# Attention with scores laid out key by query, the maximum brought in as a row of the product, and two heads on halves of TensorE's array

## The chip, the cores and the metric

The kernel runs on one core of a Trainium2 chip. The time is device microseconds (us) of one launch, median of several executions. Five engines work side by side: TensorE (PE; its loads of the stationary operand are listed as PEld), VectorE (DVE), ScalarE (ACT), GpSimd (POOL) and SyncE (SP), which issues the DMAs. TensorE multiplies a stationary operand of up to 128 contraction rows by 128 columns with a moving operand of up to 512 columns; the result lands in PSUM, in banks of 512 f32 per partition.

## The reference

A backbone of two layers over 512 latent tokens and 256 context tokens, width 1024, all in float32. Layer 0 mixes tokens by attention, layer 1 by a two-directional state-space scan; a gated convolutional feed-forward follows each. The change lies in the attention of layer 0. There are 16 heads of 64 channels and 4 key and value heads, so four query heads share one key head:

```python
def gqa_attend(q, k, v):
    s = jnp.einsum('bqhgd,bkhd->bhgqk', q, k).astype(jnp.float32) * (HEAD_DIM ** -0.5)
    p = jax.nn.softmax(s, axis=-1).astype(v.dtype)
    return jnp.einsum('bhgqk,bkhd->bqhgd', p, v)
```

Queries and keys are normalised per head, and those of latent tokens are rotated by position. The 512 latent queries attend to all 768 keys, the 256 context queries to the 256 context keys. An output projection `w_o` and a gated residual follow.

## The kernel before, in words

Activations lie channel major (channels on partitions, tokens along the free dimension). Float32 products are made from a fast, rounded format (fp32r): an operand is split into a rounded high part and a low rest (`split`, L81), and a product takes three passes, high x high, high x low, low x high (`mm3`, L100). Plain f32 products, used where the operand is not split, appear in the trace as two instructions each.

`attention` (L379) first makes queries, keys and values of the first heads in an order written out by hand, up to some 90 us. From `man.__exit__` on, the order of instructions on each engine is made by a planner: it takes the program's order as priority and, where an instruction would have to wait in its own timing, puts a later one first that is ready.

The attention proper runs over eight pairs of heads, and for each pair over three units (`Unit`): queries 0 to 255, 256 to 511 of the latents, and the context queries. A unit goes through two sets of steps, and the second set of one unit is written beside the first set of the next:

- `a_steps`: for each head `e` and each tile of 128 queries, `score` (L594) makes scores with queries on partitions and 768 (or 256) keys along the free dimension. The query operand holds the high part of a head on 64 rows and its low part on the other 64 (L562 to L566). The keys are there with their high part on both halves, and with their low part on both halves, so two passes give all four products. `softmax` (L570) takes the maximum along the row (L572), the exponential with that bias and its sum (L574), the reciprocal (L575), and scales (L576).
- `b_steps`: for each tile of 128 keys, four transposes on TensorE (L626) turn the probabilities so that keys lie on partitions; a copy out of PSUM on ScalarE or VectorE (L630); and the product with the values (L638), plain f32, one head on array columns 0 to 63 and one on 64 to 127. At the end the output is copied (L640) into a tile `o` that stays in SBUF for every pair.

Score results use the two PSUM buffers `S` of two banks each; all else uses four buffers `B` of one bank.

Between the steps `fill.run(us)` (L185) issues filling: other work that attention does not need at once, as generators that yield their cost. These are the conditioning products of layer 0 (`ada`, L111, which load 512 KB pieces of `in_adaB`), the preparation of queries of later pairs (`queries`, `normed`: product, rotation through a DMA that swaps partitions, L519, on SP, and GpSimd or VectorE, then normalisation), the second half of the keys, and, towards the end, the output projection of the first five pairs (`project`). A generator that yields `BREAK` is left alone for five calls and booked with 1.0 us. `fill.require` makes a preparation complete at that place. `osplit` splits a pair's output into its parts for the projection.

All DMAs go through SP's queue in its order; the time from issue to landing is listed in the profile.

## Time and profile before

| what | value |
|---|---|
| median of 3 runs | 1963.2 us (1959.49 to 1968.46) |
| the profiled execution | 1956.99 us, its span 1955.2 us |
| mean granted TensorE clock | 0.994 |
| score products (L594), first and last start | 94.6 and 396.3 us |
| value products (L638), first and last start | 121.9 and 418.4 us |
| busy time of L594, L626, L638 on TensorE, 92 to 425 us | 74.55, 74.92, 75.46 us |

Spans of a matrix product in the trace contain its pipeline, so that consecutive ones overlap; the distance of starts says how long one holds the engine. An entry `128*64 128x256 f32` is a product with 128 contraction rows, 64 columns of the array and 256 moving columns. In lists of groups, the number behind the bar is busy time and the mean of one instruction in ns, and then the idle time ahead of it with what ended it. In lists of waits, the columns are total us, times, longest.

### The profile page before, as it was taken

The page shows a single profiled execution, that of the slowest core. Times are in us where ns is not written, and L with a number is a line of the kernel's source. Part 1 is how long each engine was busy: PE and PEld are TensorE (multiplying, and loading weights), DVE is VectorE, ACT ScalarE, POOL GpSimd, SP SyncE. Part 2 cuts the span into 40 slices and gives each one's busy share as a digit, 9 for nine tenths or more (in the row PEclk, how much of TensorE's full clock was granted, in tenths as well). Part 3 has the DMA queues.
Part 4 walks back from the last instruction along what each step waited for, and adds up shares of the span by engine and source line. Part 5 has one row for each costly group of instructions (what it writes and reads, how often), then busy time and mean ns, then how long its engine had stood idle before and what let it go on. Part 6 is the DMA issues. An engine that isn't in the chain of part 4 may idle for free.

```text
span 1955.2 us, 28359 instructions
## 1 busy us (share of the span) xinstructions
PE 1909.6 (98%) x11068; PEld 1595.4 (82%) x11068; DVE 1346.6 (69%) x2119; ACT 885.1 (45%) x1636; POOL 297.5 (15%) x272
## 2 busy tenths in 40 slices
PE   8999999998999999999999999999999999999999
PEld 6866776688888888888888888888888888888887
DVE  4557778667877777775568777778878566555555
ACT  3645676436222222222256767666667343333331
POOL 2212201003000000000031233422335210000000
PEclk8999999999999999999999999999999999999999
DMA  8254010012434333332222433433354323333332
GB/s 330 87 183 162 28 33 17 1 55 98 143 125 123 128 124 123 123 106 65 76 87 66 134 119 108 121 116 92 103 162 119 101 74 96 97 97 97 97 98 87
DMA packets 71702, 205.36 MB, mean 105 GB/s; under 512 B 8720, under 2 KB 14224, under 8 KB 71440
## 3 DMA queue, kind: packets, MB, share of 16 engines
q1 hardware_dynamic: 71568, 203.54, 32.5%
q8 instruction: 87, 1.43, 0.3%
q14 instruction: 47, 0.39, 0.1%
HBM read 196.43 MB, written 4.46 MB: 103 GB/s over the span
## 4 chain that ended last, share of the span: by engine, by line
PE 70%; DVE 12%; issue 8%; POOL 4%; ACT 1%; DMA 1%; SPq 0%; POOLq 0%; DVEq 0%; ACTq 0%
PE ps_up L106 10%; PE ps_up L108 10%; PE ps_up L105 10%; PE ps_d L105 6%; PE ps_d L108 6%; PE ps_d L106 6%; PE ps_o L638 3%; PE ps_pt L626 3%; PE ps_s L594 2%; DVE xf L900 2%; POOL E L999 1%; DVE ht L281 1%; PE ps_in L108 1%; DVE E L1009 1%; DVE Bf L900 1%
## 5 line engine op out<-in xcount | busy, mean ns | idle before, releaser
L87 DVE TENSOR_TENSOR wl<-wst,wh 128x1024 fp32r<-128x1024 f32 x205 | 253.1, 1234 | 276.1 <-PE ps_up L106 124.1
L85 ACT CAST wh<-wst 128x1024 fp32r<-128x1024 f32 x211 | 221.1, 1049 | 413.3 <-DMA wst<-in_wup 323.7
L106 PE MATMUL ps_up<-hlf,wh 128*128 128x512 f32 x1008 | 357.0, 354 | 0.0
L105 PE MATMUL ps_up<-hhf,wh 128*128 128x512 f32 x1008 | 356.9, 354 | 0.0
L108 PE MATMUL ps_up<-hhf,wl 128*128 128x512 f32 x1008 | 356.8, 354 | 0.0
L106 PEld LDWEIGHTS ps_up<-hlf,wh 128*128 128x128 f32 x1008 | 190.6, 189 | 26.1
L105 PEld LDWEIGHTS ps_up<-hhf,wh 128*128 128x128 f32 x1008 | 190.5, 189 | 26.2
L108 PEld LDWEIGHTS ps_up<-hhf,wl 128*128 128x128 f32 x1008 | 190.5, 189 | 26.0
L105 PE MATMUL ps_in<-hhs,wh 128*128 128x512 f32 (+1 forms) x560 | 205.0, 366 | 0.0
L108 PE MATMUL ps_in<-hhs,wl 128*128 128x512 f32 (+1 forms) x560 | 199.7, 357 | 0.0
L106 PE MATMUL ps_in<-hls,wh 128*128 128x512 f32 (+1 forms) x560 | 199.5, 356 | 0.0
L105 PE MATMUL ps_d<-hdh,wh 128*128 128x512 f32 (+1 forms) x568 | 193.8, 343 | 1.4 <-DVE X L726 1.2
L108 PE MATMUL ps_d<-hdh,wl 128*128 128x512 f32 (+1 forms) x568 | 193.5, 341 | 0.0
L106 PE MATMUL ps_d<-hdl,wh 128*128 128x512 f32 (+1 forms) x568 | 193.0, 340 | 0.3 <-DVE hdl L87 0.3
L726 DVE SCALAR_TENSOR_TENSOR X<-ps_d,mod,X 128x512 f32<-128x512 f32 (+1 forms) x240 | 133.0, 584 | 31.3 <-PE ps_d L108 30.6
L106 PEld LDWEIGHTS ps_d<-hdl,wh 128*128 128x128 f32 x568 | 106.7, 188 | 15.5 <-DVE hdl L87 0.7
L105 PEld LDWEIGHTS ps_d<-hdh,wh 128*128 128x128 f32 x568 | 106.3, 188 | 15.3 <-DVE X L726 1.6
L105 PEld LDWEIGHTS ps_in<-hhs,wh 128*128 128x128 f32 x560 | 106.3, 190 | 15.1 <-issue 0.9
L108 PEld LDWEIGHTS ps_in<-hhs,wl 128*128 128x128 f32 x560 | 106.2, 190 | 14.9
L108 PEld LDWEIGHTS ps_d<-hdh,wl 128*128 128x128 f32 x568 | 106.7, 188 | 13.3
L106 PEld LDWEIGHTS ps_in<-hls,wh 128*128 128x128 f32 x560 | 106.3, 190 | 13.6
L167 DVE SCALAR_TENSOR_TENSOR junk<-wada,cb 128x1024 f32<-128x1024 f32 x96 | 116.7, 1215 | 1.1 <-ACT cb L159 0.9
(325 smaller groups left out, 3699.7 us busy)
## 6 DMA issues: line engine op xcount, KB each, us to landing
wst<-in_wup SPq DMA_DIRECT2D x88, 512.0 KB, 3.5
wada<-in_adaT SPq DMA_DIRECT2D x48, 512.0 KB, 3.5
wst<-in_win SPq DMA_DIRECT2D x48, 512.0 KB, 3.5
wst<-in_wdown SPq DMA_DIRECT2D x44, 512.0 KB, 4.1
wada<-in_adaB SPq DMA_DIRECT2D x32, 512.0 KB, 7.4
E<-ad SPq DMA_DIRECT2D x64, 256.0 KB, 6.5
ec<-ead SPq DMA_DIRECT2D x64, 128.0 KB, 4.3
wst<-in_wout SPq DMA_DIRECT2D x16, 512.0 KB, 3.5
```

The source lines that it names most:

```text
L85: keep(nc.scalar.copy(hi, src))
L87: keep(eng.tensor_tensor(lo, src, _r(hi), ALU.subtract))
L105: mm(out, wh, ah, start=first, stop=False)
L106: mm(out, wh, al, start=False, stop=False)
L108: mm(out, wl, ah, start=False, stop=last)
L167: g.tc.keep_in_program_order(nc.vector.scalar_tensor_tensor(junk, w, 1.0, cb[:, v * D : (v + 1) * D], ALU.mult, ALU.mult, accum_out=md[:, ...
L281: nc.vector.scalar_tensor_tensor(t[:, c0:c1], ap, g.moda[layer][ca][:, m, v : v + 1], rs[:, c0:c1], ALU.mult, ALU.mult)
L594: nc.tensor.matmul(ps[:, c0 : c0 + n], qprep[self.p][e][:, q0 : q0 + P], kk[:, self.k0 + c0 : self.k0 + c0 + n], start=i == 0, stop=i == 1)
L626: nc.tensor.transpose(ps[:, e * 256 + t * P : e * 256 + (t + 1) * P], self.pr[e, t][:, kt * P : (kt + 1) * P], g.ident)
L638: nc.tensor.matmul(po[S64[e], :256], v, pts[kt - 1][:, e * 256 : (e + 1) * 256], start=kt == 1, stop=kt == nkt)
L726: nc.vector.scalar_tensor_tensor(ap, o[:, c0:c1], gate[:, m, v : v + 1], ap, ALU.mult, ALU.add)
L900: nc.vector.scalar_tensor_tensor(cv, raw[:, tap : tap + n], par(f"sw{tap}", j), cv, ALU.mult, ALU.add)
```

## The change

Pairs are no longer cut into units. Each pair takes seven steps (`Pair.steps`), and each step makes scores with keys on partitions and queries along the free dimension: six tiles of 128 keys by 512 latent queries, and in the seventh step two tiles of context keys by 256 context queries. The two heads of the pair lie on rows 0 to 63 and 64 to 127 of the array (contraction over 64 channels), each writing its own PSUM bank; three passes (high keys x high queries, low x high, high x low). A fourth product per head, of one contraction row, adds the negative maximum of each query, which lies as a row `mrow` on partition 0 or 64. The exponential then needs no bias, one instruction takes both heads (128x1024), and its result serves the value product as it is. The sum over keys is added up on VectorE over steps and finished by a product with ones (`final`); the output is divided by it through logarithm, exponential and one correction step.

The maxima come from a pass of their own (`Pair.maxima`), written among the steps of the pair before: scores with queries on partitions from the high parts alone, the two heads again on halves of the rows, a maximum over 1024 elements, and then DMAs on SP that write the column of maxima to DRAM and read it back as a row on one partition. For the first pair it is written among the products of the values.

Queries are split into two full tiles `qh`, `ql`. Outputs of the first six pairs are stored to DRAM and loaded again for `osplit`. The pool of general tiles has 18 instead of 27 buffers, with tags of their own for `pr`, `acc`, `mrow` and `o`, which at the start hold weight slabs. The order of the filling and its cost per call differ.

```diff
+    spare = [("pr", 3, 1024)] * 3 + [("acc", 1, 1024)] + [("mrow", 2, T)] * 2 + [("o", 2, T)] * 2
+    def slab_tile(name):
+        if not spare:
+            return t3(g, name, F32R)
+        tag, bufs, n = spare.pop(0)
+        return g.t3p.tile([P, n], F32R, tag=tag, bufs=bufs, name=name)[:, :W6]
...
-        slabs[k] = hi, lo = t3(g, "wsh", F32R), t3(g, "wsl", F32R)
+        slabs[k] = hi, lo = slab_tile("wsh"), slab_tile("wsl")
...
-        out = []
-        for e in range(2):
-            a = t3(g, f"q{p}{e}", F32R)
-            s, o = S64[e], S64[1 - e]
-            nc.scalar.copy(a[s], qs[s])
-            nc.vector.tensor_tensor(a[o], qs[s], _r(a)[s], ALU.subtract)
-            out.append(a)
-        qprep[p] = out
+        qprep[p] = t3(g, "qh", F32R), t3(g, "ql", F32R)
+        split(g, qs, *qprep[p])
...
-    def softmax(pr, ps):
-        mx = g.p.tile([P, 1], F32, tag="mx", bufs=4, name="mx")
-        nc.vector.reduce_max(mx, ps, axis=AX.X, negate=True)
-        sm = g.p.tile([P, 1], F32, tag="sm", bufs=4, name="sm")
-        nc.scalar.activation(pr, ps, AF.Exp, bias=mx, accum_out=sm)
-        nc.vector.reciprocal(sm, sm)
-        nc.vector.tensor_scalar(pr, pr, sm, None, ALU.mult)
...
+    onesr = g.const.tile([P, P], F32R, name="onesr")
+    nc.scalar.copy(onesr, g.ones)
+    small = lambda name, dt=F32: g.p.tile([P, 2, T // P], dt, tag="mx", bufs=6, name=name)
+    class Pair:
+        def __init__(self, p):
+            self.p, self.kv = p, p // 2
+            self.todo = []
+        def maxima(self):
+            qh, kh = qprep[self.p][0], k2[self.kv][0]
+            lat, ctx, mx = small("ma"), small("mb"), small("mx", F32R)
+            self.mrow = g.t3p.tile([P, T], F32R, tag="mrow", bufs=2, name=f"mrow{self.p}")
+            def scores(ts, k0, n, out):
+                ps = Sb("ps_m")
+                for i, t in enumerate(ts):
+                    for e in range(2):
+                        nc.tensor.matmul(ps[:, 512 * e + n * i : 512 * e + n * i + n], qh[S64[e], t * P : (t + 1) * P],
+                                         kh[S64[e], k0 : k0 + n], start=True, stop=True)
+                nc.vector.reduce_max(out[:, :, ts[0] : ts[-1] + 1], ps.rearrange("p (e t k) -> p e t k", e=2, k=n),
+                                     axis=AX.X, negate=True)
+            def row(t0, t1):
+                for e in range(2):
+                    dr = g.dp.tile([1, T], F32, tag="mrow", bufs=4, name="mrow_d")
+                    c = slice(t0 * P, t1 * P)
+                    nc.sync.dma_start(dr[0, c].rearrange("(t p) -> p t", p=P), _r(mx[:, e, t0:t1]))
+                    nc.sync.dma_start(_r(self.mrow[64 * e : 64 * e + 1, c]), dr[:, c])
+            for t in (0, 2):
+                scores((t,), 0, L, lat)
+                yield
+                scores((t + 1,), 0, L, lat)
+                yield
+                scores((t, t + 1), L, C, ctx)
+                yield
+            nc.vector.tensor_tensor(mx[:, :, :4], lat[:, :, :4], ctx[:, :, :4], ALU.min)
+            row(0, 4)
+            scores((4, 5), L, C, lat)
+            nc.vector.tensor_copy(mx[:, :, 4:], lat[:, :, 4:])
+            row(4, 6)
+            yield
+        def steps(self):
+            (qh, ql), (kh, kl) = qprep[self.p], k2[self.kv]
+            po = acc = None
+            o = g.t3p.tile([P, T], F32, tag="o", bufs=2, name=f"o{self.p}")
+            def values(po, pr, t, off, n, first, last):
+                v = vt[t][:, self.kv * HD : (self.kv + 1) * HD]
+                for e in range(2):
+                    nc.tensor.matmul(po[S64[e], :n], v, pr[:, 512 * e + off : 512 * e + off + n], start=first, stop=last)
+            def final(po, ps, acc, out):
+                n = out.shape[-1]
+                for e in range(2):
+                    nc.tensor.matmul(ps[S64[e], :n], g.ones[:, :HD], acc[:, n * e : n * e + n], start=True, stop=True)
+                y, u = t2("y")[:, :n], t2("u")[:, :n]
+                nc.scalar.activation(y, ps, AF.Ln)
+                nc.scalar.activation(y, y, AF.Exp, scale=-1.0)
+                nc.vector.tensor_tensor(out, po, y, ALU.mult)
+                nc.vector.scalar_tensor_tensor(u, ps, -1.0, y, ALU.mult, ALU.mult)
+                nc.vector.scalar_tensor_tensor(out, u, 2.0, out, ALU.add, ALU.mult)
+            def later_lat(po, pr, t, acc):
+                values(po, pr, t, 0, L, t == 0, t == 5)
+                if t == 5:
+                    final(po, Bk("ps_sum"), acc, o[:, :L])
+            def later_ctx(pr, acc):
+                pc = Bk("ps_oc")
+                for t in range(2):
+                    values(pc, pr, 4 + t, C * t, C, t == 0, t == 1)
+                final(pc[:, :C], pc[:, C:], acc, o[:, L:])
+                if self.p < 6:
+                    nc.sync.dma_start(odram[self.p], o)
+            prev = None
+            for t in range(7):
+                ps, pr = Sb("ps_s"), g.t3p.tile([P, 1024], F32, tag="pr", bufs=3, name="pr")
+                for q0, n, k0, off in (((0, L, t * P, 0),) if t < 6 else ((L, C, L, 0), (L, C, L + P, C))):
+                    q, k = slice(q0, q0 + n), slice(k0, k0 + P)
+                    outs = [ps[:, 512 * e + off : 512 * e + off + n] for e in range(2)]
+                    for i, (a, b) in enumerate(((kh, qh), (kl, qh), (kh, ql))):
+                        for e in range(2):
+                            nc.tensor.matmul(outs[e], a[S64[e], k], b[S64[e], q], start=i == 0, stop=False)
+                    for e in range(2):
+                        r = slice(64 * e, 64 * e + 1)
+                        nc.tensor.matmul(outs[e], onesr[r], self.mrow[r, q], start=False, stop=True)
+                nc.scalar.activation(pr, ps, AF.Exp)
+                if t == 0:
+                    po = Bk("ps_o")
+                elif t == 1:
+                    acc = g.t3p.tile([P, 1024], F32, tag="acc", bufs=1, name="acc")
+                    nc.vector.tensor_tensor(acc, prev, pr, ALU.add)
+                elif t < 6:
+                    nc.vector.tensor_tensor(acc, acc, pr, ALU.add)
                 else:
+                    acc = t2("accc")
+                    halves = pr.rearrange("p (e k q) -> p e k q", e=2, k=2)
+                    nc.vector.tensor_tensor(acc.rearrange("p (e q) -> p e q", e=2), halves[:, :, 0], halves[:, :, 1], ALU.add)
+                prev = pr
+                yield (lambda t=t, pr=pr, po=po, acc=acc: later_lat(po, pr, t, acc)) if t < 6 else (
+                    lambda pr=pr, acc=acc: later_ctx(pr, acc))
+            g.o.append(o)
...
+    odram = [g.dp.tile([P, T], F32, name=f"odram{p}") for p in range(6)]
...
     def osplit(p):
         hl_, hc_ = htiles(g, L, f"ol{p}"), htiles(g, C, f"oc{p}")
+        o = g.o[p]
+        if p < 6:
+            o = t3(g, f"od{p}")
+            nc.sync.dma_start(o, odram[p])
+        split(g, o[:, :L], *hl_)
+        split(g, o[:, L:T], *hc_)
+    adas = list(fill.q)
+    fill.q = [kgen if o == "k" else adas.pop(0) if o == "a" else qgen[int(o)] for o in "12a3a4ka5a6a7aaa"]
+    pairs = [Pair(p) for p in range(NH // 2)]
+    m = pairs[0].maxima()
+    for i, _ in enumerate(vals):
+        if i % 6 == 5:
+            next(m, None)
+            next(qgen[1], None)
+    for _ in m:
+        pass
+    late_step = None
+    for p in range(NH // 2):
+        m = iter(())
+        if p < 7:
+            fill.require(qgen[p + 1])
+            if p == 3:
                 fill.require(kgen)
+            m = pairs[p + 1].maxima()
+        us = .8 if p < 6 else 1.45
+        for t, todo in enumerate(pairs[p].steps()):
+            next(m, None)
+            fill.run(us)
+            if late_step:
+                late_step()
+            late_step = todo
+            if t == 0:
+                next(m, None)
+                if p == 6:
+                    for i in range(5):
+                        osplit(i)
+                    late()
+            if p == 7 and t == 3:
+                osplit(5)
+                osplit(6)
+            fill.run(us)
+    late_step()
...
-    g.t3p, g.n3 = pool("pa", pha), 27
+    g.t3p, g.n3 = pool("pa", pha), 18
+    g.dp = pool("adram", pha, space=bass.MemoryType.DRAM)
```

More of the change, by code (lines that the diff above doesn't have):

```diff
@@ L673, in attention @@
-    fill.q = [vals] + [kgen if o == "k" else adas.pop(0) if o == "a" else qgen[int(o)] for o in "a1aa2aa3aaa4k567"]
+    adas = list(fill.q)
+    fill.q = [kgen if o == "k" else adas.pop(0) if o == "a" else qgen[int(o)] for o in "12a3a4ka5a6a7aaa"]
     g.o = []
-    units = [Unit(p, hf) for p in range(NH // 2) for hf in range(3)]
-    for n in range(len(units) + 1):
-        A = units[n] if n < len(units) else None
-        B = units[n - 1] if n else None
-        if n == 1:
-            fill.q.remove(vals)
-            for i, _ in enumerate(vals):
-                if i % 8 == 8 - 1:
-                    for p in range(1, 2):
-                        next(qgen[p], None)
-        if A and A.hf == 0:
-            g.o.append(t3(g, f"o{A.p}"))
-            if A.p:
-                fill.require(qgen[A.p])
-            if A.p == 4:
-                fill.require(kgen)
-            if A.p == 7:
-                for p in range(6):
-                    osplit(p)
-                late()
-        a, b = (A.a_steps() if A else iter(())), (B.b_steps() if B else iter(()))
-        while True:
-            ra, rb = next(a, 0), next(b, 0)
-            if ra == rb == 0:
-                break
-            fill.run((.65, 1.3)[0] if n < 21 else (.65, 1.3)[1])
-        if n == 22:
-            osplit(6)
```

60 lines of the change are left out of this document (removed).

## The prediction, made before the result was known

> **What bounds the kernel now.** I read the shares of the page first, then busy time by stretch, then the order of TensorE's instructions in the attention stage, then who waits for whom there, last the DMA queue.
>
> ```profile
> PE 1909.6 (98%) x11068; PEld 1595.4 (82%) x11068; DVE 1346.6 (69%) x2119; ACT 885.1 (45%) x1636; POOL 297.5 (15%) x272
> ...
> 110.00:425.00 315.00, 307.81 (x1968) 211.25 (x1967) 224.50 (x441) 176.26 (x369) 42.11 (x27) 0.99 0.21 70
> ```
>
> The columns of the second row are stretch, length, busy time of PE, PEld, DVE, ACT and POOL, granted clock, DMA share, GB/s. From 110 to 425 us the kernel does attention, with other products as filling. TensorE is busy 307.81 of 315 us; VectorE 224.50, ScalarE 176.26. The clock is 0.99, so no gain can come from it. What counts in this stage is how long TensorE needs from one start to the next:
>
> ```profile
> 122.50 0.66 PE L626 MATMUL ps_pt<-cst,pr 128*128 128x128 f32 x4
> 122.92 0.47 PE L594 MATMUL ps_s<-kh,q 128*128 128x512 f32 x1
> ...
> 344.49 0.50 PE L594 MATMUL ps_s<-kh,q 128*128 128x512 f32 x1
> 344.83 0.39 PE L594 MATMUL ps_s<-kl,q 128*128 128x512 f32 x1
> 345.06 0.28 PE L594 MATMUL ps_s<-kh,q 128*128 128x256 f32 x1
> 345.18 0.28 PE L594 MATMUL ps_s<-kl,q 128*128 128x256 f32 x1
> 345.38 0.65 PE L638 MATMUL ps_o<-pT,v 128*64 128x256 f32 x2
> 345.96 0.66 PE L626 MATMUL ps_pt<-cst,pr 128*128 128x128 f32 x4
> 346.55 0.65 PE L638 MATMUL ps_o<-pT,v 128*64 128x256 f32 x4
> 347.13 0.66 PE L626 MATMUL ps_pt<-cst,pr 128*128 128x128 f32 x4
> ```
>
> Columns: start, extent, instruction. A score product of 512 columns takes 0.23 us from start to start (344.83 to 345.06), of 256 columns 0.12 (345.06 to 345.18), four transposes 0.42, so 0.105 each (122.50 to 122.92). The value products (L638) write 64 partitions each; two heads have half of the array's columns each, and each product is two passes, so four instructions per round (this trace lacks two of them at 345.38). They hold TensorE for 0.58 us (346.55 to 347.13). Whether halves of the array work side by side is seen from these rows:
>
> ```profile
> 1420.15 1.89 PE L966 MATMUL ps_st<-xw,Bt 128*128 128x256 f32 x8
> 1421.69 0.47 PE L105 MATMUL ps_in<-hhs,wh 128*128 128x256 f32 x1
> ...
> 115.50 1.85 PE ps_ada L128 x16
> ```
>
> A pass of 256 columns of the same plain f32 kind over the whole array takes 1.54/8 = 0.19 us, so one of 512 columns 0.38. The conditioning products (L128, 512 columns, four groups of 32 array columns) take 1.85/16 = 0.12 each: groups of columns do run side by side. So a round of value products streams for 2 x 0.19 = 0.38 of its 0.58 us. The other 0.20 is the change of the array's division. Around it, 345.18 to 345.38 takes 0.20 where 0.12 is usual, and the first product after a change takes 0.34 (344.49 to 344.83) where 0.23 is usual. One trip into divided columns and back thus costs 0.20 + 0.08 + 0.11 = 0.39; part of the 0.20 may be streaming, so I use **0.35 per trip, 0.17 per change of division**.
>
> **The change, part by part.** What goes and what stays is counted here:
>
> ```profile
> L594 PE MATMUL ps_s<-kh,q x128: 277/386/504, 94.6 to 378.9; 128*128 128x512 f32 x64, 128*128 128x256 f32 x64
> ...
> L594 PE MATMUL ps_sc<-kh,q x32: 277/368/561, 131.4 to 396.0; 128*128 128x256 f32 x32
> ...
> L626 PE MATMUL ps_pt<-cst,pr x384: 270/273/476, 114.9 to 406.3; 128*128 128x128 f32 x192
> ...
> L626 PE MATMUL ps_pt<-cst,prc x64: 270/272/329, 151.3 to 414.3; 128*128 128x128 f32 x64
> ...
> L638 PE MATMUL ps_o<-pT,v x448: 379/379/690, 121.9 to 418.4; 128*64 128x256 f32 x150
> ```
>
> The kl products are as many as the kh ones. *Removed:* 448 transposes x 0.105 = 47 us. 128 score products of 512 columns x 0.23 and 192 of 256 x 0.12 = 52.5 us. *Added, per head pair, if the two heads run side by side on halves of the array's rows:* key-major scores, three passes in six steps of 512 columns and twice three of 256: 18 x 0.23 + 6 x 0.12 = 4.9; the row of maxima as a product with one contraction row: 6 x 0.23 + 2 x 0.12 = 1.6; the query-major pass from which the maxima come: 4 x 0.23 + 6 x 0.12 = 1.6. Together 8.1, times 8 pairs 65 us. The value products stream the same number of columns, so they cancel. The sums are one more product with halves of columns over 512 and 256 columns: 2 x 0.38 + 2 x 0.19 = 1.14, so 9 us for 8 pairs. Streaming: -47 - 52.5 + 65 + 9 = **-25.5 us**.
>
> *Trips into a divided array:* before, 448 / 4 = 112. After, values 7 per pair, and 8 blocks of row-half products per pair (7 steps, and one more since two pieces of the maxima come in step 0): 120. 8 x 0.35 = **+3**.
>
> *Row halves* do not occur before. Bounds: side by side as the column groups, which is the sum above, or one after the other: then the 65 us double. I take the first, since division by columns is the nearest row. The Trainium skill (TensorEngine Tiling (Array Packing), Key Properties) says that tiles operate independently, which would give the same sum; no row here shows it for rows of the array. The skill's TensorE: Matmul & The Clock Gate (Part 3, measured speedup) has 3.07 times for four row tiles rather than four; an estimate from it would stretch the 65 us to 85.
>
> *The maximum's row* contracts over one partition, at 0 and at 64. If that is another division than the 64-row halves, each of the 56 steps pays two changes more: 112 x 0.17 = 19 us. If it is not, 0. Filling is absent in part of the slots, since a generator's break is booked as 1.0 us there without a product: then halves of rows and halves of columns follow each other with one change instead of two. So between 0 and 19 I take the middle, **+10**. The same Tiling page says that a change of tiling mode, not of tile, drains the engine. The trace agrees where it can, with the 0.58 us for 0.38 us of streaming.
>
> *The old softmax chain* (maximum, exponential, sum, reciprocal, scaling, transposes, copies) let TensorE wait:
>
> ```profile
> PEld ps_s L594 <- ACT pr L574: 5.2, 10, 1.0
> ...
> PEld ps_pt L626 <- DVE pr L576: 1.9, 4, 0.9
> ...
> PE ps_s L594 <- ACT pr L574: 1.7, 3, 0.8
> ...
> PEld ps_s L594 <- ACT prc L574: 1.3, 2, 1.1
> ```
>
> These are 10 us; after, values come a whole step behind their exponentials, so I take **-8**.
>
> *VectorE and ScalarE* stay off the path:
>
> ```profile
> L572 DVE TENSOR_REDUCE mx<-ps_s 128x1 f32<-128x768 f32 x64 | 60.6, 952 | 10.5 <-PE ps_s L594 10.0
> L576 DVE TENSOR_SCALAR pr<-pr,sm 128x768 f32<-128x768 f32 x64 | 40.1, 626 | 0.8
> L630 DVE COPY pT<-ps_pt 128x512 f32<-128x512 f32 x37 | 25.3, 683 | 8.8 <-PE ps_pt L626 8.5
> ...
> L575 DVE RECIPROCAL sm<-sm 128x1 f32<-128x1 f32 x96 | 15.0, 157 | 10.9 <-ACT pr L574 6.9 <-ACT prc L574 3.5
> L572 DVE TENSOR_REDUCE mx<-ps_sc 128x1 f32<-128x256 f32 x32 | 13.2, 418 | 5.2 <-PE ps_sc L594 5.1
> L576 DVE TENSOR_SCALAR prc<-prc,sm 128x256 f32<-128x256 f32 x32 | 12.9, 407 | 0.6
> ...
> L630 ACT COPY pT<-ps_pt 128x512 f32<-128x512 f32 x75 | 43.4, 587 | 56.1 <-PE ps_pt L626 52.5 <-issue 3.2
> ...
> L87 DVE TENSOR_TENSOR wl<-wst,wh 128x1024 fp32r<-128x1024 f32 x205 | 253.1, 1234 | 276.1 <-PE ps_up L106 124.1
> ```
>
> VectorE loses 167 us (sum of its six rows). A maximum over 1024 elements, by (952 - 418)/512 = 1.04 ns each, takes 1.22: 56 make 68 us. 40 additions of 1024 elements at 1.23 (L87) and 8 of 512 at 0.68 make 55. The five-instruction division by sums has three on VectorE, 8 x 3 x (0.68 + 0.42) = 26. Together 149, so VectorE stays near 207 of 315 us. ScalarE loses 43 us of copies. Neither ends the stage; price 0. The storing of six outputs to DRAM and their reload is a pair or more ahead of its use; price 0, and some 3 us each were the cover gone.
>
> *The maxima's way into a row* is the new wait. For each pair eight DMAs go over SP: column to DRAM, DRAM to one partition, for two heads and two parts.
>
> ```profile
> L519 SPq DMA_DIRECT2D qsw<-qs x16: 507/588/601, 221.4 to 324.5; - x16
> ...
> DMA to landing us min/median/max: 1.9/2.0/3.8
> ...
> wada<-in_adaB SPq DMA_DIRECT2D x32, 512.0 KB, 7.4
> ...
> x<-xd SPq DMA_DIRECT2D x16, 128.0 KB, 2.9
> ...
> 148.69 20.07 SPq L122 DMA_DIRECT2D wada<-in_adaB  x10
> ```
>
> The critical part (latent queries) is two writes and two reads: 1.2 issue + 2.0 landing + 1.2 issue + 2.9 landing = 7.3 us. Writes of single f32 elements occur nowhere before; 2.0 is the nearest row, 7.4 (landing between large loads) the far end. The minimum is issued in step 5 of a pair, and the row is needed at the end of the scores of the next pair's step 0. A step is 315/56 = 5.6 us, so one and a half steps are 8.4 us: just hidden. While SP waits for a first write to land, loads of weights and of the rotation (L519) stand behind it; they are due a pair later. For pair 0 nothing covers it but the filling that can be put ahead: of 7.3 us I take **+5**.
>
> **Sum.** -25.5 + 3 + 10 - 8 + 5 = -15.5. The profiled execution took 1957.0 us (span 1955.2), so 1941.5; the median of the runs shown, 1963.2, is 6.2 above it. Forecast: 1948 us.
>
> **Rivals.** *The row comes late* (ends slower). If element writes land as the loads between other loads do, the chain is 1.2 + 7.4 + 1.2 + 7.4 = 17 us, 9 more than its cover. Conditioning loads are spread over some five of the seven pairs that follow another: 5 x 9 = 45, so 1948 + 45 = 1993. It decides from 3 us of lateness per pair on (15.5/5). For it speaks the 20 us that SP needed for ten loads; against it that the planner puts ready products ahead of a waiting one, and that nothing loads after 200 us but w_o. *Row halves run one after the other:* + 65, so 2013. Nothing in the trace speaks for it but that it is not there. *The changes of division eat the gain:* the row at its upper end (+9 over mine) and the maxima in trips of their own, since their buffer is still held by a reduction (56 x 0.35 = +20): 1948 + 29 = 1977, or 1968 with half of the trips. This is what the Tiling page's rule about the drain would do here.
>
> **How the numbers follow.** 0.5% of 1963 is 10 us, about what a measurement of this kernel can tell from no change. Chances: forecast 0.47 (its own range, with the row at 0 and no wait at pair 0 at the low end, 1933, and some lateness at the high end, 1962); late row 0.24; cancelled by changes 0.20; one after the other 0.09. Faster: 0.42 of the first and 0.05 of those cases where the others are mild, 0.47. Same: 0.05 of the first, 0.12 of the third, 0.04 of the second, 0.21. Slower: 0.32. The range goes from 1930 to 1993, which leaves out the last case.
>
> **What would show it.** Row-half products of two heads that start within 0.02 us of each other, and groups of six score products of some 0.7 us, show the first step right. Changes show as 0.17 us at the borders of the blocks. In the waits, products with the maximum's row waiting for a DMA beyond 3 us per pair show the late row. The attention stretch should be some 300 instead of 315 us long, and everything behind it only moved. The forecast is wrong if row halves are serial, if the maxima stand in trips of their own, or if preparation of queries, needed now for the maxima a pair earlier, holds TensorE.

## The result, and the profile after

The changed kernel takes 2019.8 us (median of 4 runs, 2015.6 to 2026.0) against 1963.9 of the kernel before: 1.029 times, with a 95% interval of 1.025 to 1.033. The forecast was 1948 us, and the range up to 1993 did not hold the time. The profiled execution took 2016.5 us, its span 2014.7.

The page of the changed kernel: the granted clock in 40 slices of 50 us, the packets, and the chain that ended last, by engine and by line:

```profile
PEclk8979789799999999999999999999999999999999
...
DMA packets 86290, 210.13 MB, mean 104 GB/s; under 512 B 21744, under 2 KB 27264, under 8 KB 86032
...
PE 69%; DVE 12%; DMA 7%; issue 4%; POOL 2%; ACT 2%; SPq 0%; POOLq 0%; DVEq 0%; ACTq 0%
PE ps_up L105 10%; PE ps_up L106 10%; PE ps_up L108 10%; PE ps_d L105 6%; PE ps_d L106 6%; PE ps_d L108 6%; DMA mrow_d<-mx 3%; PE ps_in L108 2%; PE ps_in L105 2%; PE ps_in L106 2%; DVE xf L951 2%; PE ps_o L628 2%; PE ps_s L664 1%; DMA wst<-in_wq 1%; DVE ht L281 1%
```

Packets and chain by engine on the page of the kernel before:

```profile
DMA packets 71702, 205.36 MB, mean 105 GB/s; under 512 B 8720, under 2 KB 14224, under 8 KB 71440
...
PE 70%; DVE 12%; issue 8%; POOL 4%; ACT 1%; DMA 1%; SPq 0%; POOLq 0%; DVEq 0%; ACTq 0%
```

The clock is below full speed up to some 400 us, which it was not before. There are 13,024 more packets under 512 bytes; the maxima alone are 8 pairs x 2 heads x 768 = 12,288 single elements. DMA has risen from 1% to 7% of the chain, and the largest part of it is the write of the maxima to DRAM. So the page already points at the new transfers, but not at how they do harm.

Where the time is lost shows in the first product of the feed-forward (tile `ps_up`), which starts when attention and its projection are done. Here from the listing of that tile, of before and then of after; first and last start stand behind the three durations:

```profile
L105 PE MATMUL ps_up<-hhf,wh x1008: 277/389/398, 480.1 to 1939.1; 128*128 128x512 f32 x112, 128*128 128x256 f32 x56
```

```profile
L105 PE MATMUL ps_up<-hhf,wh x1008: 277/389/632, 534.6 to 1998.8; 128*128 128x512 f32 x112, 128*128 128x256 f32 x56
```

54.5 us are lost by then. Behind it, up to the end of the span, it is 1475.1 us before and 1480.1 after. Single traces differ there by more than that for reasons that have nothing to do with the change: the experiments below leave all code behind attention as it was, and lie between 1478.3 and 1488.1.

Stretches of the attention stage of the changed kernel (length, busy time of PE, PEld, DVE, ACT, POOL, granted clock, DMA share, GB/s), then two short ones:

```profile
92.00:130.00 38.00, 28.66 (x211) 23.91 (x213) 19.83 (x26) 10.21 (x20) 7.63 (x6) 0.90 0.37 35
130.00:200.00 70.00, 67.00 (x356) 33.27 (x349) 40.15 (x53) 24.66 (x32) 15.69 (x8) 0.88 0.42 96
200.00:300.00 100.00, 85.01 (x421) 44.43 (x421) 50.09 (x63) 30.06 (x41) 14.04 (x8) 0.81 0.27 56
300.00:400.00 100.00, 95.30 (x494) 47.99 (x490) 63.27 (x87) 37.58 (x54) 9.88 (x6) 0.88 0.43 111
```

```profile
208.00:216.00 8.00, 0.96 (x2) 0.45 (x2) 0.00 (x0) 1.75 (x2) 0.63 (x1) 0.50 0.87 55
220.00:230.00 10.00, 10.00 (x35) 5.32 (x35) 7.86 (x13) 1.95 (x4) 3.83 (x3) 0.50 0.28 95
```

From 92 to 400 us TensorE is idle for 32 us (9.3 + 3.0 + 15.0 + 4.7), and the clock costs up to 43 us more (each length by one less its clock, the idle part included). The last two rows show the two together: 7 of 8 us idle at half clock, and then full occupation, still at half clock. What stopped TensorE there shows in the timeline of all engines (start, extent, instruction; in brackets the idle time ahead of it and what ended it; `x2` stands for two like instructions):

```profile
208.53 0.96 PE L667 MATMUL ps_s<-mrow,onesr 1*128 1x512 f32 x2 [1.86 <-DMA mrow<-mrow_d]
...
214.25 1.04 ACT L85 CAST wh<-wst 128x1024 fp32r<-128x1024 f32 x1 [15.49 <-DMA wst<-in_wq]
215.20 1.02 ACT L668 ACTIVATE pr<-ps_s 128x1024 f32<-128x1024 f32 x1
216.27 0.79 PE L593 MATMUL ps_m<-kh,qh 64*128 64x512 f32 x2 [6.78 <-ACT pr L668]
```

TensorE had its row of maxima at 208.53 and finished those scores. The exponential that must free the score buffer stood on ScalarE behind a cast of query weights (L85), and that cast waited 15.49 us for its load. In the queue of SP that load lies right behind the writes of maxima:

```profile
195.02 0.93 SPq L602 DMA_DIRECT2D mrow_d<-mx  x2
...
197.45 0.35 SPq L95 DMA_DIRECT2D wst<-in_wq  x1
```

Issued at 197.45, used at 214.25: 16.8 us for 512 KB. The waits of this kernel (total us, times, longest):

```profile
PE ps_s L667 <- DMA mrow<-mrow_d: 17.8, 7, 8.5
...
ACT wh L85 <- DMA wst<-in_wq: 24.9, 2, 15.5
...
SPq L603 <- DMA mrow_d<-mx: 135.5, 24, 10.2
```

TensorE itself waits for the row only 17.8 us, 8.5 of them at pair 0. SP waits 135.5 us until writes of maxima have landed, 5.6 each time. Two explanations were open: TensorE's wait for a late row, or the harm that these DMAs do to others; and beside them, that the new attention has no gain to show in the first place.

### The profile page after: what moved, and what is told of

It is laid out like the page before. It is cut to its first block, busy times and chain, and to the rows that moved or that the text cites. A ratio compares the mean times of both kernels' runs of the same rounds, so it can differ in the third digit from the quotient of the medians.

```text
span 2014.7 us, 27655 instructions
## 1 busy us (share of the span) xinstructions
PE 1941.6 (96%) x10844; PEld 1565.3 (78%) x10844; DVE 1333.2 (66%) x1954; ACT 825.0 (41%) x1426; POOL 300.2 (15%) x272
## 4 chain that ended last, share of the span: by engine, by line
PE 69%; DVE 12%; DMA 7%; issue 4%; POOL 2%; ACT 2%; SPq 0%; POOLq 0%; DVEq 0%; ACTq 0%
PE ps_up L105 10%; PE ps_up L106 10%; PE ps_up L108 10%; PE ps_d L105 6%; PE ps_d L106 6%; PE ps_d L108 6%; DMA mrow_d<-mx 3%; PE ps_in L108 2%; PE ps_in L105 2%; PE ps_in L106 2%; DVE xf L951 2%; PE ps_o L628 2%; PE ps_s L664 1%; DMA wst<-in_wq 1%; DVE ht L281 1%
## 5 line engine op out<-in xcount | busy, mean ns | idle before, releaser
L85 ACT CAST wh<-wst 128x1024 fp32r<-128x1024 f32 x211 | 221.0, 1048 | 456.5 <-DMA wst<-in_wup 324.8
```

The source lines that it names most:

```text
L85: keep(nc.scalar.copy(hi, src))
```

## The experiments

Kernels were measured in sets, each beside runs of the kernel before of its own; its medians there are 1965.2 us (the kernels without a transport, with longer runs, with the row by products and with the old DMAs unread), 1969.6 (writes alone, 64 rows, the best) and 1962.8 (the cast taken off ScalarE, and the kernel before with writes). Where two kernels of different sets are compared, their difference is given by the medians and by the ratios to before, and the two differ by some 5 us.

**The new attention without the transport of the maxima.** A tile `flat`, filled once with -8, takes the place of the row.

```diff
-            self.mrow = g.t3p.tile([P, T], F32R, tag="mrow", bufs=2, name=f"mrow{self.p}")
+            self.mrow = flat
...
             def row(t0, t1):
-                for e in range(2):
-                    dr = g.dp.tile([1, T], F32, tag="mrow", bufs=4, name="mrow_d")
...
+                pass
...
-                nc.scalar.activation(pr, ps, AF.Exp)
+                nc.scalar.activation(pr, ps, AF.Exp, scale=1 / 64)
```

> This kernel leaves out the transport of the maxima: no DMA of the column to DRAM and back. The row is a constant, and the exponential has a scale so that values stay finite; scores, maxima, reductions and all products stay. Theory A (the row comes late: TensorE idles on it, and its clock falls to half after each idle stretch): in the changed kernel's trace about 35 us of idle time of TensorE from 92 to 480 us and about 33 us at half clock hang on it, so 1950 to 1962 us, granted clock from 0.81 to 0.88 back to 0.98 or more in the stage. Theory B (changes of the array's division and the extra products cost the time; without this wait another takes its place): 2000 us or more.

Measured: 1971.3 us, 1.001 of before (0.9995 to 1.003). Its stretches:

```profile
92.00:130.00 38.00, 37.37 (x268) 28.49 (x270) 22.94 (x32) 16.12 (x26) 9.99 (x7) 0.96 0.29 96
130.00:200.00 70.00, 70.00 (x412) 36.79 (x412) 48.52 (x67) 27.09 (x38) 19.56 (x11) 0.98 0.30 98
200.00:300.00 100.00, 99.61 (x572) 51.76 (x570) 66.90 (x85) 40.96 (x55) 12.48 (x7) 1.00 0.23 72
300.00:400.00 100.00, 96.93 (x523) 54.12 (x519) 67.44 (x97) 35.93 (x51) 4.86 (x3) 0.93 0.28 93
```

48 us come back by the medians, 54 by the ratios, and with them TensorE's occupation and clock. So the way of the maxima, with the waiting for it, is most of the loss. But the kernel stays level with before: the forecast without a wait at pair 0 was 1943, so a gain of some 20 us is missing as well.

**The row by products instead of DMAs.** Each column of 128 maxima goes through TensorE against the unit matrix into one row, and ScalarE copies it.

```diff
             def row(t0, t1):
+                for t in range(t0, t1):
+                    for e in range(2):
+                        nc.tensor.matmul(ps[64 * e : 64 * e + 1, (t - t0) * P : (t - t0 + 1) * P], mx[:, e, t : t + 1],
+                                         g.ident, start=True, stop=True)
                 for e in range(2):
-                    dr = g.dp.tile([1, T], F32, tag="mrow", bufs=4, name="mrow_d")
...
+                    nc.scalar.copy(self.mrow[64 * e : 64 * e + 1, c], ps[64 * e : 64 * e + 1, :n])
```

> The column is brought into a row by TensorE (12 products per pair of one stationary column with the unit matrix, about 1.5 us per pair or 12 us in all) and two ScalarE copies, with no DMA. Theory A: 1955 to 1972 us, at most 15 above the kernel without transport. Theory B: 2000 us or more.

Measured: 1983.3 us, 1.010 of before (1.007 to 1.013). That is 12 us over the kernel without a transport, which is the price of these products and copies: in this trace the products alone hold TensorE for 11.9 us by the distances of their starts. It is 36 us under the changed kernel.

**The same, with the old DMAs issued as well** and their result read by nobody (`mdum`).

```diff
+                for e in range(2):
+                    dr = g.dp.tile([1, T], F32, tag="mrow", bufs=4, name="mrow_d")
+                    nc.sync.dma_start(dr[0, c].rearrange("(t p) -> p t", p=P), mx[:, e, t0:t1])
+                    nc.sync.dma_start(_r(self.mdum[64 * e : 64 * e + 1, c]), dr[:, c])
```

> As the kernel whose row comes by TensorE, with the old DMAs still issued, to DRAM and back into a tile that nobody reads (one general buffer less for it). What it costs over that kernel is what the DMAs do to others: SP held until a write has landed, loads and rotations behind it, rings filled with single elements. Theory A (TensorE's direct wait for the row is most of it): at most 15 us over it. Theory C (what stands behind the DMAs is most of it): 30 us or more over it, that is 1990 us or more.

Measured: 2026.5 us, 1.032 of before (1.028 to 1.036). 43 us are back, although TensorE no longer waits for any of these DMAs. In the waits of this kernel ScalarE does, longer than in the changed kernel:

```profile
ACT wh L85 <- DMA wst<-in_wq: 39.9, 3, 14.4
```

So most of the harm is not the late row; it is that other loads come late. That may be since SP is held at the reads, or since the writes themselves are slow. For the tile `mdum` this kernel and the next two have 17 general buffers instead of 18; no run shows what that costs by itself.

**The writes alone, without the reads back.**

```diff
-                    nc.sync.dma_start(_r(self.mdum[64 * e : 64 * e + 1, c]), dr[:, c])
```

> As the kernel whose row comes by TensorE with the old DMAs still issued, but without the reads back: the same single-element writes go to DRAM, and no DMA on SP waits any more for a write to land. The pair of kernels differed by 43 us with and without the DMAs. Theory C1 (SP is held: what stands behind the read on its queue comes late): 1980 to 1992 us. Theory C2 (the single elements fill the rings that the loads use): 2015 to 2030 us.

Measured: 2017.5 us, 1.025 of before (1.022 to 1.027), so 29 (ratios) to 34 us (medians) of the 43 remain. SP now has no read to hold back, though it still stands, with loads behind, until the maxima are there (94 us over the stage). That this alone costs the 29 to 34 is unlikely: the kernel with longer pieces, below, stands for 74 us and is only 13 us over the one without a transport. This kernel has the landing of its DMAs on record (the issues: KB, median us to landing; the row above them is for the tile of the maxima, least, median, most):

```profile
DMA to landing us min/median/max: 8.9/11.1/18.1
...
mrow_d<-mx SPq DMA_DIRECT2D x16, 2.0 KB, 11.1
...
mrow_d<-mx SPq DMA_DIRECT2D x16, 1.0 KB, 11.0
...
wst<-in_w_o SPq DMA_DIRECT2D x8, 512.0 KB, 10.2
```

and the kernel without any of these writes:

```profile
wst<-in_w_o SPq DMA_DIRECT2D x8, 512.0 KB, 4.1
```

2 KB of single elements take 11.1 us to land, no more than 1 KB, and a 512 KB load beside them 10.2 instead of 4.1. The Trainium skill (DMA: Bandwidth & Descriptors, Queues, rings and completion order) says that each DMA engine takes the descriptors of a ring in order. By that a load would wait behind the elements; whether it waits there or at the memory stays open (below). The stop of TensorE from the last section is still there, by the same load:

```profile
201.72 0.34 SPq L95 DMA_DIRECT2D wst<-in_wq  x1
...
213.95 1.05 ACT L85 CAST wh<-wst 128x1024 fp32r<-128x1024 f32 x1 [9.49 <-DMA wst<-in_wq]
```

**The late load taken off ScalarE.** As the last, with the query weights split by GpSimd alone, so that no exponential stands behind the waiting cast. The load itself stays as late: from its issue to the cast the first of these loads takes 18.6 us in both kernels, the third 12.2 and 12.5.

```diff
-            w = load_w(g, I["wq"][p - 4], lo_engine="pool")
+            nc.sync.dma_start(st, I["wq"][p - 4])
+            nc.gpsimd.tensor_copy(wh, st)
+            nc.gpsimd.tensor_tensor(wl, st, _r(wh), ALU.subtract)
```

> As the kernel with the row by TensorE and the single-element writes still issued (no reads), but the weights of the later queries are split on GpSimd alone, so that ScalarE's queue no longer waits for their load. In that kernel ScalarE stood 30.7 us in three waits for these loads, with exponentials behind. Theory D (the loads, late behind the single elements, stop ScalarE, and through the exponentials TensorE): 30.7 us and what the clock loses after each stop, so 1975 to 1995 us instead of 2017. Rival E (TensorE itself needs the late weights for its filling, or other loads take the same place): 2005 us or more.

Measured: 1995.0 us, 1.016 of before (1.014 to 1.018): 17 us less by the ratios and 22 by the medians, with the same writes. From 200 to 300 us, the kernel before this edit and then with it:

```profile
200.00:300.00 100.00, 91.69 (x534) 48.42 (x536) 56.32 (x73) 39.86 (x60) 14.14 (x8) 0.91 0.23 57
```

```profile
200.00:300.00 100.00, 98.51 (x590) 51.45 (x587) 67.23 (x82) 41.33 (x61) 18.69 (x13) 0.98 0.36 94
```

This shows the larger part of what the writes cost as one chain: late load, ScalarE's cast, the exponentials behind it, TensorE, its clock.

**Longer runs in the same DMAs.** The queries of the maxima's pass are taken with a stride, so that four (two) maxima of a partition are neighbours in the row, and the writes consist of 16- and 8-byte pieces.

```diff
-                    nc.sync.dma_start(dr[0, c].rearrange("(t p) -> p t", p=P), _r(mx[:, e, t0:t1]))
+                    nc.sync.dma_start(dr[0, c].rearrange("(p t) -> p t", p=P), _r(mx[:, e, t0:t1]))
```

> The maxima pass takes every fourth (context: every second) query in a tile, so that a partition's maxima are neighbours in the row: the writes to DRAM are 128 runs of 16 (8) bytes instead of 512 (256) of 4 bytes, as many DMAs and waits as before. Theory A1 (the number of single elements makes the write slow): the write's landing falls from about 10 us to 3 or 4 and the time to 1955 to 1975 us. Theory A2 (the trip through DRAM is slow by itself, whatever the pieces): 2010 to 2025 us.

Measured: 1984.3 us, 1.010 of before (1.007 to 1.013). SP's wait in it:

```profile
SPq L608 <- DMA mrow_d<-mx: 33.7, 22, 4.7
```

SP waits 1.5 us each time instead of 5.6, with the same bytes, and 35 us by the medians (37 by the ratios) are gone. What is slow is the division into single elements, not the way over DRAM. The pieces are here both fewer and longer, so which of the two counts is not told apart. It is 10 us above what was expected, so these DMAs are still not free.

**The row over 64 contraction rows.** In the kernel with the row by products, the product that adds the maximum contracts over all 64 rows of its head, 63 of them zero, so that the division of the array stays.

```diff
-                        r = slice(64 * e, 64 * e + 1)
+                        r = S64[e]
                         nc.tensor.matmul(outs[e], onesr[r], self.mrow[r, q], start=False, stop=True)
```

> The kernel whose row comes by TensorE, with the row's product contracted over the head's 64 rows (zeros below the maximum) instead of one row, so that it stays in the division of the scores. It takes away the 112 changes of division around the row. If the row's product pays them: 112 x 0.10 to 0.17 = 11 to 19 us less than the 1983 us of that kernel, 1964 to 1972 us. If a product of one row is in the same division as the 64-row halves, or the changes are hidden: 1980 us or more.

Measured: 1968.4 us, 1.000 of before (0.998 to 1.001): 15 us less by the medians, 20 by the ratios, where 11 to 19 were expected. TensorE's timeline, with the row (L667 in the changed kernel, L676 here) among its neighbours; first the changed kernel:

```profile
313.48 0.39 PE L664 MATMUL ps_s<-qh,kl 64*128 64x512 f32 x2
313.71 0.40 PE L664 MATMUL ps_s<-ql,kh 64*128 64x512 f32 x2
314.04 0.49 PE L667 MATMUL ps_s<-mrow,onesr 1*128 1x512 f32 x2
314.46 0.51 PE L593 MATMUL ps_m<-kh,qh 64*128 64x512 f32 x2
```

```profile
305.22 0.39 PE L673 MATMUL ps_s<-qh,kl 64*128 64x512 f32 x2
305.45 0.40 PE L673 MATMUL ps_s<-ql,kh 64*128 64x512 f32 x2
305.68 0.39 PE L676 MATMUL ps_s<-mrow,onesr 64*128 64x512 f32 x2
305.91 0.40 PE L599 MATMUL ps_m<-kh,qh 64*128 64x512 f32 x2
```

Each pair of products (`x2`, one per head) takes 0.23 us, so the halves of the rows run side by side. Around a row of one contraction row it is 0.33 + 0.42, over 64 rows 0.23 + 0.23: two changes cost 0.29 us. Each pair makes eight such rows and not seven, since the seventh step has two tiles of context keys. That is 19 us for 64 rows at most, less where a change falls there anyhow, and 16 us for the 56 that were counted ahead.

**The best of these.** The kernel of the last experiment, with the splits of the first five outputs for the projection (`osplit`) spread over five steps of the seventh pair rather than issued in one.

```diff
-                if p == 6:
-                    for i in range(5):
-                        osplit(i)
-                    late()
+            if p == 6 and t < 5:
+                osplit(t)
+                if t in (2, 4):
+                    late((0, 1, 2) if t == 2 else (3, 4))
```

> The 64-row contraction, the row by TensorE, and the preparation of the first five pairs' outputs for the projection spread over five steps of the seventh pair instead of all in its first step. In the kernel without transport some 10 us of half clock and idle time lay at 320 to 346 us, behind that block of ScalarE and VectorE work. If so: 5 to 10 us less than without the spreading, 1955 to 1966 us, at or below the kernel before (1965). If the time there has another cause: the same as without the spreading within 3 us.

Measured: 1966.4 us (12 runs), 0.998 of before (0.996 to 0.9999). The stretch 300 to 400 us, without and with the edit:

```profile
300.00:400.00 100.00, 92.45 (x555) 54.82 (x554) 65.59 (x95) 37.52 (x56) 5.88 (x3) 0.91 0.26 88
```

```profile
300.00:400.00 100.00, 95.47 (x585) 55.25 (x583) 68.56 (x96) 41.22 (x60) 5.69 (x3) 0.98 0.28 91
```

TensorE's stops and the clock mend in this trace, but its execution took 1960.6 us where the median is 1966.4, and the medians of the two kernels differ by 2 us where 5 to 10 were expected. That is within the 3 us of the other theory, so it is not shown that the splits cost this time. The kernel is 0.2% under the kernel before, less than the 0.5% that a measurement of it can tell from no change.

**The kernel before, with such writes.** Each of its 96 columns of maxima is also written to DRAM, 128 single elements each, and nobody reads them.

```diff
-        mx = g.p.tile([P, 1], F32, tag="mx", bufs=4, name="mx")
+        mx = g.p.tile([P, 1], F32, tag="mx", bufs=24, name="mx")
         nc.vector.reduce_max(mx, ps, axis=AX.X, negate=True)
+        dr = g.dp.tile([1, P], F32, tag="mrow", bufs=24, name="mrow_d")
+        nc.sync.dma_start(dr[0, :].rearrange("(t p) -> p t", p=P), mx)
```

> The kernel before, with one addition: each column of maxima (128 f32, 96 of them, 12288 single elements in all, as many as in the changed kernel) is also written to DRAM with single elements, and nobody reads it. If the harm lies in the DMAs themselves, whatever the attention looks like: 1985 to 2010 us. If it needs the new order of the filling (loads spread over all pairs, due soon): 1965 to 1975 us, since before, the loads are mostly issued by 200 us and due late.

Measured: 2172.2 us, 1.105 of before (1.101 to 1.110), far beyond what either theory gave. SP's waits for VectorE in it:

```profile
SPq L574 <- DVE mx L572: 197.1, 46, 12.2
```

It shows that such DMAs harm without anything of the new attention. Its size isn't a price of the writes: there are 96 DMAs instead of 32 for the same number of elements, and SP also stands for 197 us before them until VectorE has the next column, with loads behind. How much of it comes from the writes and how much from SP's standing was not told apart.

The start of the first feed-forward product, as above, in each trace, against the 480.1 us of before:

| kernel | first `ps_up` | against before | median us |
|---|---|---|---|
| changed kernel | 534.6 | +54.5 | 2019.8 |
| no transport of maxima | 483.3 | +3.2 | 1971.3 |
| pieces of 16 and 8 bytes | 500.1 | +20.0 | 1984.3 |
| row by products | 497.8 | +17.7 | 1983.3 |
| and old DMAs, unread | 550.1 | +70.0 | 2026.5 |
| and old writes alone | 529.4 | +49.3 | 2017.5 |
| writes alone, weights split on GpSimd | 512.7 | +32.6 | 1995.0 |
| row by products, 64 rows | 487.1 | +7.0 | 1968.4 |
| and `osplit` spread | 475.7 | -4.4 | 1966.4 |
| before, with writes | 696.5 | +216.4 | 2172.2 |

It orders the kernels nearly as the medians do: what tells them apart lies up to the end of attention.

## Why the prediction was wrong

*Streaming, -25.5: right, as far as the traces show.* The products of attention (scores, transposes, values) kept TensorE busy for 224.9 us before, from 92 us to their end. In the kernel without the transport (three passes; row; maxima; values, and sums of the latent and of the context queries) it is

```profile
92.00:470.00 378.00, 56.89 (x384) 30.66 (x384) 0.97 0.24 79
92.00:470.00 378.00, 30.31 (x128) 12.02 (x128) 0.97 0.24 79
92.00:470.00 378.00, 28.28 (x160) 13.13 (x160) 0.97 0.24 79
92.00:470.00 378.00, 66.01 (x256) 14.22 (x256) 0.97 0.24 79
92.00:470.00 378.00, 14.20 (x64) 4.97 (x64) 0.97 0.24 79
```

That is 195.7 us. Busy time contains the overlap of neighbours. What the products hold TensorE for is seen better from each start to the next, without idle time, and with what the granted clock cost of it (each stretch times one less its clock). Added up in the two traces to the start of `ps_up`:

| up to the first `ps_up` | before: us, of it the clock's | without the transport: us, of it the clock's |
|---|---|---|
| products of attention | 185.1, 2.8 | 176.5, 6.7 |
| all other products | 275.1, 5.5 | 287.9, 12.0 |
| TensorE idle | 18.9, 0.2 | 17.9, 0.1 |

At full clock the products of attention gain 12.5 us (182.3 against 169.8) and the others lose 6.3 (269.6 against 275.9), together 6.2. The prediction's terms give 3.5 to 6.5, with the row as it was paid (25.5 less 3 for trips and 16 to 19 for the row). From 92 us on, the other products border on a change of division 222 times instead of 91, as none of attention's products uses the undivided array any more; that this is why they take longer is likely, but no run shows it.

*Row halves side by side: right.* The heads of a pair start together, and a pair takes the time of one product. The rival of one after the other (2013) was close to the measured time by chance only. What the Trainium skill says of independent tiles (TensorEngine Tiling (Array Packing), Key Properties) is what the rows show. The Trainium skill's 3.07 for four row tiles rather than four (TensorE: Matmul & The Clock Gate, Part 3, measured speedup) is not tested here; with two halves no such loss shows.

*Changes of division: right in kind, mis-sized.* The row was put between 0 and 19 and taken as +10; paid were 16 to 19 by the timeline, 15 to 20 by the runs. That is 5 to 10 more.

*The old softmax chain, -8: mis-sized, and given back.* Stretches of the kernel before:

```profile
92.00:110.00 18.00, 16.95 (x133) 16.18 (x133) 10.91 (x21) 9.13 (x19) 2.03 (x2) 1.00 0.07 17
110.00:200.00 90.00, 88.65 (x613) 55.78 (x611) 59.86 (x119) 46.22 (x95) 20.82 (x12) 0.98 0.53 188
200.00:300.00 100.00, 98.33 (x629) 69.92 (x628) 73.98 (x148) 67.14 (x142) 16.65 (x12) 0.98 0.10 27
300.00:400.00 100.00, 95.83 (x580) 66.83 (x581) 75.56 (x154) 56.32 (x124) 4.64 (x3) 1.00 0.03 9
```

TensorE is idle there for 8 us for whatever reason (1.05 + 1.35 + 1.67 + 4.17), and the clock costs 4. Without the transport it is idle for 4 (0.63 + 0.39 + 3.07, above), and the clock costs 10. So 4 of the 8 came, and 6 were lost, most of them between 300 and 400 us, where the clock was 0.93 instead of 1.00. Up to the first `ps_up` only 1 us of idle time is left of the gain, by the table. Nor were 8 there to be had: the 10 us that the prediction added up are mostly waits of PEld, and PE can still be busy while a load waits. PE's own idle time, from 92 to 440 us, is

```profile
L626 PE MATMUL ps_pt<-cst,pr 128*128 128x128 f32 x384 | 65.2, 287 | 1.1 <-DVE pr L576 1.1
L594 PE MATMUL ps_s<-kh,q 128*128 128x512 f32 (+1 forms) x128 | 46.8, 367 | 3.7 <-ACT pr L574 1.7 <-DVE q L565 1.1 <-ACT prc L574 0.9
```

so 3.7 us wait for exponentials and scaling (1.1 + 1.7 + 0.9).

The prediction asked what would be late next in other places and not here. The splits of five outputs in one step may be part of it: with them spread, the trace has the stretch mended, but the medians do not show the gain.

*The maxima's way into a row: the step that failed.* It took 2.0 us for the landing of a write of single elements, from `qsw`, and 7.4 as the far end. Such a write took 11.1 us in the kernel with the writes alone. The nearest row was near in its queue and not in its shape: rows of whole partitions against elements. The rival of the late row used 7.4 as well, and had the harm in the wrong place, at TensorE's own wait. That wait was 17.8 us, and the writes without any reader still cost 29 to 34.

*"loads of weights and of the rotation (L519) stand behind it; they are due a pair later", without a price: the second failure, and the dearer one.* Among the writes, loads came 6 us and more late (10.2 instead of 4.1, and 18.6 instead of 4.2 from issue to cast for the first load of query weights), and the first who waited was ScalarE, at a cast. The prediction had asked who is queued behind the wait on SP, and not who is queued behind the cast on ScalarE: the exponentials. Also *VectorE and ScalarE, price 0*, was therefore right for their busy time and wrong for their order.

*The clock, "no gain can come from it": right, but a loss could.* Around the stop of 7 us at 208 it was 0.50, and still in the 10 us of full occupation from 220 on.

*Everything behind it only moved:* right within what single traces of that code differ (1478.3 to 1488.1 us).

Of the 56 us, then, the way of the maxima accounts for 48 to 54 (the changed kernel against the one without it). Most of that is loads that come late: 29 to 34 of 43 us in the kernels that differ in the writes alone, 17 to 22 of these through ScalarE's cast; the rest, 9 to 14, comes with the reads, at which SP is held. The 43 and the 29 to 34 may contain what the one buffer less costs in the kernels with `mdum`.

Even without the way of the maxima the gain of some 20 us (15.5, and the 5 of pair 0) is missing: in the traces that kernel starts `ps_up` 3.2 us behind. By the table above, products at full clock gain 6.2 and idle time 0.9, and the clock loses 10.3 (18.8 against 8.5), 3 of them before 92 us, where the last products of keys start at 93.2 instead of 90.3. So the failed terms are here the row, 5 to 10 us too low, the softmax chain, 7 too high, and the clock, which was put at nothing and cost 10. These are single traces, and why the clock falls in that kernel was not taken apart.

Open, too, is why single elements land so slowly, and no more slowly at 512 than at 256, and whether the loads wait for them in the rings or at the memory. The packet records of the writes alone narrow this: two writes of 256 elements, issued at 199.8 and 200.2 us, have all their packets, of 9 ns each, behind them at 202. Then no packet starts until 205, and the 4096-byte packets of the loads behind take up to 3.8 us each until 210, where 0.16 is the median. So it is not the sending of the elements that takes the time; what holds the packets behind them, the records do not say.

## What to carry to other kernels

Don't price a DMA by its bytes alone: one that is cut into single elements landed after 11 us here for 1 or 2 KB. And look for the loads around it: a transfer that nobody waits for delayed them too. For each load that may come late, find the engine that waits first, and then what stands behind that instruction in the same engine's order; here a cast of weights ahead of exponentials turned a late load into an idle TensorE, at half clock. A column on partitions is turned into a row more cheaply by TensorE (12 us for eight pairs here) than by single-element DMAs (some 50), and where the array is divided, a short product was better padded with zeros to the division in use (15 to 20 us here).

## What the runs showed of the hardware that was not expected

- A write of 256 or of 512 single f32 elements from SBUF to DRAM landed after 11.0 and 11.1 us (8.9 to 18.1), where the rotation's transfer in the kernel before took 2.0. In 16- and 8-byte pieces SP's wait for it fell from 5.6 to 1.5 us.
- The 512 KB loads of `w_o` took 10.2 us in a kernel with such writes, instead of 4.1 without; 6.6 in a second kernel with the same writes, whose stage ran otherwise.
- Products of one contraction row between products of 64 cost two changes of division, 0.29 us; with the same product over 64 rows there was none.
- Two products on the two halves of the rows took 0.23 us for 512 columns, no longer than one product of the same format over the whole array in the kernel before.
- Around a stop of 7 us TensorE was granted 0.50 of its clock, and this lasted over the whole of the stretch from 220 to 230 us, though it was busy all the time.
